# The SwiGLU product's blocks stored as high and low parts

## The chip, the cores and the metric

The kernel runs on one core of a Trainium2 chip. The metric is the device time of one execution in microseconds (us). Before the change three runs took 2479.89 to 2483.35 us, median 2483.05 us.

## The reference, cut to what matters

Two decoder layers act on x of shape 1024 x 1024 in float32. Each has a mixer, a cross attention into 256 memory tokens and a SwiGLU feed-forward stage, each followed by a layer norm of `ALPHA * x + f(x)`. The feed-forward stage is the one that the change touches:

```python
def swiglu_ffn(x, w_gate, w_up, w_down):      # w_gate, w_up: 1024 x 2816; w_down: 2816 x 1024
    return (jax.nn.silu(x @ w_gate) * (x @ w_up)) @ w_down
```

## The kernel before, in words

**Three matmuls for one.** Every float32 operand of a large product is split into a high part (a cast on ScalarE, ACT, to the rounded type float32r) and a low part (operand minus high part, on VectorE, DVE, or GpSimd, POOL). TensorE (PE) then does low*high, high*low and high*high into the same bank (`mm3`, L209 to L212). `split` (L214 to L216) makes the two parts.

**Seven products for eight.** Both matmul stages of the feed-forward use a two-by-two block scheme with seven block products; the operands of some of the seven are sums and differences of blocks.

**Gate and up stage** (`ffn`). The 22 feature chunks of 128 are worked through in 11 pairs c, one row chunk from each half. For one c, seven block products give the gate and seven give the up values, each of 12 matmuls (128x128 by 128x512). `operands` and `operand` make the weight operand of a product up to four products ahead (`while len(made) < min(4, left)`): DVE sums and differences (L1130 to L1139), an ACT cast (L1112), a DVE subtraction (L1113). `finish` empties the bank: ACT copies and silu, DVE additions and the product `hf`. Once all four blocks of `hf` exist, `store` (L1153) lets POOL make four sums and differences of 128x512 (L1159 to L1162); the seven resulting blocks go to DRAM, tile `hD`, in four transfers issued on ACT. These are deferred by `later` and `emit_later`, which runs once per block product here and once per group in the down stage.

**Down stage** (`ffn_down`, `seven`). The seven block products are taken in the order 1, 5, 6, 3, 7, 4, 2. Each is a block of six groups g (two feature chunks each, the last has one), and a group is 24 matmuls: 4 output tiles x 2 chunks x 3. A block product has 132 matmuls, the stage 924. For each group `operands7` takes the `hD` block by a load on SyncE's queue (SP; tile `raw`, in a pool of four buffers), has ACT cast it (`dh<-raw`, L215) and POOL subtract (`dl<-raw`, L216). It takes the weight block (`down_B`, tile `wp`): for products 1, 5, 6 and 4 a load of `in_wd`; for 5, 6, 7 and 4 a DVE difference of 128x1024 (L777, L783, L780, L786); then an ACT cast (`dh<-wp`) and a DVE subtraction (`dl<-wp`). The lookahead `look(j)` is 4 groups, 6 in products 4 and 2. During product 1 and 5 a `hook` also scales and shifts the eight residual tiles x (L1337, L1338), five on DVE and three on POOL.

**Order.** The order on each engine is that of the code, each engine works its queue in order, and semaphores join them. Everything but the residual pools lives in 44 pages of 4 KB per partition, and an instruction that writes a page waits for the last use of it.

Of the kernel before, what the change touches and what calls it, by code (L numbers as in the profile page):

```python
# [7 lines left out]
F32 = mybir.dt.float32  # L8
F32R = mybir.dt.float32r
# [6 lines left out]
P = 128  # L16
# [58 lines left out]
class Weights:  # L75
# [7 lines left out]
        self.split_ahead = 1  # L83
        self.lo_engine = ("vector",)

    def add(self, src, shape, scale=None, raw=False, page=False):
        self.items.append(dict(src=src, shape=shape, scale=scale, keep=raw or page, page=page))

    def load(self, parts=None):
        k, it = self.k, self.items[self.loaded]  # L90
        if it["page"]:
            it["raw"] = k.page(f"wp{self.loaded}", it["shape"])
        else:
            it["raw"] = k.raw.tile([P] + it["shape"], F32, tag="raw", name=f"raw{self.loaded}")
        if parts is None:
            k.nc.sync.dma_start(it["raw"], it["src"])
        else:
            for c in parts:
                k.nc.sync.dma_start(it["raw"][:, c, :], it["src"][:, c, :])
        self.loaded += 1  # L100
        return it["raw"]
# [43 lines left out]
class Kern:  # L145
    def __init__(self, ctx, tc, a):
        self.tc, self.nc, self.a = tc, tc.nc, a
        nc = self.nc
        self.pool = ctx.enter_context(tc.tile_pool(name="pages", bufs=a["n_pages"]))
        self.raw = ctx.enter_context(tc.tile_pool(name="rawp", bufs=4))  # L150
        dram = ctx.enter_context(tc.tile_pool(name="dram", bufs=1, space=bass.MemoryType.DRAM))
        self.xD = [dram.tile([P, D], F32, name=f"xD{t}") for t in range(NT)]
        self.hD = [dram.tile([7, P, min(2, HF - c), 512], F32, name=f"hD{c}") for c in range(0, HF, 2)]
        self.memT = [dram.tile([P, 4, MEM], F32, name=f"memT{q}") for q in range(2)]
        self.tmp = ctx.enter_context(tc.tile_pool(name="tmp", bufs=4))
        self.small = ctx.enter_context(tc.tile_pool(name="small", bufs=16))
        self.cst = ctx.enter_context(tc.tile_pool(name="cst", bufs=1))
        self.psum = ctx.enter_context(tc.tile_pool(name="psum", bufs=8, space=bass.MemoryType.PSUM))
        self.n = 0
        self.w = Weights(self)  # L160
        self.bg = []
        self.bg2 = []
        self.bg3 = []
        self.credit = [0.0, 0.0]
        self.later = []
        self.AT = [None, None]
# [937 lines left out]
    def ffn(self, layer):  # L1104
# [47 lines left out]

        def store(c, h):  # L1153

            a11, a21, a12, a22 = h[0][:, 0, :], h[0][:, 1, :], h[1][:, 0, :], h[1][:, 1, :]
            s12, s34 = self.page("s12", [2, 512]), self.page("s34", [2, 512])
            s1, s2, s3, s4 = s12[:, 0, :], s12[:, 1, :], s34[:, 0, :], s34[:, 1, :]
            gp = nc.gpsimd.tensor_tensor
            gp(s1, a21, a22, op=ALU.add)  # L1159
            gp(s3, a11, a21, op=ALU.subtract)  # L1160
            gp(s2, s1, a11, op=ALU.subtract)
            gp(s4, a12, s2, op=ALU.subtract)  # L1162
            dst = self.hD[c // 2][:, :, c % 2, :]

            def put(lo, src):
                return lambda: nc.scalar.dma_start(dst[lo:lo + src.shape[1]].rearrange("s p n -> p s n"), src)

            later.extend([(0, put(0, h[0][:, 0:1, :])), (0, put(1, h[1])), (3, put(3, s12)), (4, put(5, s34))])

        def finish(m, st, i, j, add, bank):  # L1170

# [126 lines left out]


    def down_operands(self):  # L1300
        return self.operands7(ORDER_D, lambda j, g: self.w.take(), self.down_B(self.nc.vector), len(self.hD))

    def ffn_down(self, layer):
        nc = self.nc
        self.w.split_ahead = 0
        self.w.lo_engine = ("gpsimd",)
        x = self.x = [None] * NT
        sts = [self.sm("lst", 5) for _ in range(NT)]
        gb, gx = [], []

        def norm_b(t):
            self.ln_b(x[t], sts[t], gb)
            if layer == DEPTH - 1:
                nc.sync.dma_start(self.a["out"][t * P:(t + 1) * P, :], x[t])

        def add(j, p, b):
            if j == 2 and p:
                norm_b(p - 1)
            self.add_block(j, b, x[p], x[p + 4], sts[p], sts[p + 4])
            if j == 4:  # L1320
                self.ln_a(x[p + 4], sts[p + 4])
            if j == 2:
                self.ln_a(x[p], sts[p])
                if layer < DEPTH - 1 and p < 2:
                    self.w.ahead(2 * p + 2, 2 * p + 4)

        def hook(j, g):
            self.emit_later()
            if j == 1 and g < 4:
                for t in (g, g + 4):  # L1330
                    x[t] = self.page("x", [D])
                    nc.sync.dma_start(x[t], self.xD[t])
            if j == 1 and g == 0:
                gx.extend(self.ln_params(self.a["ln_xa_g"][layer], self.a["ln_xa_b"][layer]))
            for t, eng in AFFINE.get((j, g), ()):
                eng = getattr(nc, eng)
                eng.tensor_tensor(x[t], x[t], gx[0], op=ALU.mult)  # L1337
                eng.tensor_tensor(x[t], x[t], gx[1], op=ALU.add)  # L1338
            if j == 4 and g == 0:
                gb.extend(self.ln_params(self.a["ln_ffn_g"][layer], self.a["ln_ffn_b"][layer]))  # L1340
            if j == 2 and 1 <= g < 5:
                norm_b(3 + g)

        self.seven(ORDER_D, self.down_made, self.down_ops, len(self.hD), HF, lambda j: 6 if j in (4, 2) else 4, add, hook, 1)
        self.down_ops = self.down_made = None
        self.last = (x[3], sts[3], gb)
        if layer == DEPTH - 1:
            x, st = x[3], sts[3]
            nc.vector.scalar_tensor_tensor(x, x, st[:, 2:3], gb[0], op0=ALU.add, op1=ALU.mult)
            for i, q in enumerate((nc.scalar, nc.sync)):  # L1350
                sl = slice(i * 512, i * 512 + 512)
                nc.vector.scalar_tensor_tensor(x[:, sl], x[:, sl], st[:, 4:5], gb[1][:, sl], op0=ALU.mult, op1=ALU.add)  # L1352
                q.dma_start(self.a["out"][3 * P:4 * P, sl], x[:, sl])
# [60 lines left out]
    def plan(self):  # L1414
        a, w = self.a, self.w

        def mem_k(l, extra=None, at=8):
            for q in range(2):
                w.add(self.memT[q], [4, MEM])
            for i in range(8):  # L1420
                if i == at:
                    extra()
                w.add(a["wk"][l, i], [8, P])

        def wout(eh):
            for kp in range(4):
                w.add(a["w_out"][eh, kp], [2, 512], page=True)

        def mem_v(l):
            for i in range(8):  # L1430
                w.add(a["wv"][l, i], [8, P])

        def attn(l):
            for i in range(8):
                w.add(a["wqT"][l, i], [8, P])
            for i in range(8):
                w.add(a["xa_wo"][l, i * P:(i + 1) * P, :], [D])

        def ffn(l):
            for c in range(2):  # L1440
                w.add(a["wg"][l, HF * c], [8, P])
                w.add(a["wu"][l, HF * c], [8, P])
            for m in range(2, NFF):
                for r in range(2):
                    w.add(a["wg" if m % 2 == 0 else "wu"][l, m // 2 + HF * r], [8, P], raw=True)
            for j in ORDER_D:
                for g, h in enumerate(self.hD):
                    w.add(h[DOWN_A[j]], [min(2, HF - 2 * g), 512], raw=True)
                    if j in DOWN_B:
                        r, c = DOWN_B[j]  # L1450
                        w.add(a["wd"][l, r, c, :, 2 * g:min(2 * g + 2, HF), :], [min(2, HF - 2 * g), 512], page=True)

        for i in range(24):
            w.add(a["w_in"][i], [8, P])
        mem_k(0, lambda: wout(0), 7)
        wout(1)
        for q in range(2):
            w.add(self.memT[q], [4, MEM])
        mem_v(0)
        attn(0)  # L1460
        ffn(0)
        mem_k(1)
        for i in range(2):
            w.add(a["pool_w"][i], [4, 256], (lambda i: lambda: self.pscale[:, i * 512:(i + 1) * 512].rearrange(
                "p (g c) -> p g c", c=256).unsqueeze(2).broadcast_to([P, 2, 2, 256]))(i))
        mem_v(1)
        attn(1)
        ffn(1)
# [120 lines left out]
```

## Time and profile before

| | |
|---|---|
| median of three runs | 2483.05 us |
| profiled execution | 2486.67 us, its span 2484.9 us |
| PE busy | 2325.7 us (94%) |
| DVE busy | 1842.3 us (74%) |
| ACT busy | 1050.7 us (42%) |
| POOL busy | 1044.8 us (42%) |
| DMA | 263.27 MB, mean 106 GB/s |

PE is the busiest engine, and its matmuls are pipelined: one is shown with 0.39 us but the next starts about 0.227 us later. So the time of a stage is read from the starts of its first and last matmul, not from busy time. An idle time is shown in brackets with the instruction that ended it. [...]

### The profile page before, as it was taken

Reading aid. Unit: us, or ns where it says so; the run is one execution under the profiler, and the core shown is the slowest. Engines: PE = TensorE matmul, PEld = TensorE weight load, DVE = VectorE, ACT = ScalarE, POOL = GpSimd, SP = SyncE. Lnnn points to the kernel's source line nnn. Section 1 sums busy time; section 2 is a strip of 40 time slices with the busy share of each in tenths; the row PEclk is TensorE's granted clock in tenths of the full one; section 3 lists DMA queues with packets and bytes.
Section 4 is the critical chain, followed back from the end, with each engine's and each line's share of the span. In section 5 each row is a group of like instructions: output and inputs, shape, how many; then the busy total and the mean of one; then the engine's idle time right before and its main releaser. Section 6 shows DMA issues by size and latency. Waiting matters only on the chain. (4 is left out here: it accounts for less than half of the span.)

```text
span 2484.9 us, 29326 instructions
## 1 busy us (share of the span) xinstructions
PE 2325.7 (94%) x11208; PEld 1920.4 (77%) x11208; DVE 1842.3 (74%) x1950; ACT 1050.7 (42%) x1723; POOL 1044.8 (42%) x573
## 2 busy tenths in 40 slices
PE   8999997798979999999989989798999999998997
PEld 6777776696868888888768789686788888886776
DVE  6986789877895766666788856979676666668877
ACT  3254564354736433333324443455454333332433
POOL 1332446666582112122556574666611211218654
PEclk9999999899989999999999999899999999999999
DMA  4211133150212133332734342302113323346342
GB/s 182 68 34 35 34 109 137 35 179 25 85 43 94 68 107 107 101 110 94 289 134 145 126 153 94 110 10 97 66 62 109 116 85 106 111 145 253 131 158 88
DMA packets 84476, 263.27 MB, mean 106 GB/s; under 512 B 8432, under 2 KB 8944, under 8 KB 84336
## 3 DMA queue, kind: packets, MB, share of 16 engines
q1 hardware_dynamic: 58464, 203.97, 24.2%
q10 hardware_dynamic: 25872, 57.42, 6.1%
q8 instruction: 89, 1.46, 0.3%
q14 instruction: 51, 0.42, 0.1%
HBM read 198.97 MB, written 62.39 MB: 105 GB/s over the span
## 5 line engine op out<-in xcount | busy, mean ns | idle before, releaser
L210 PE MATMUL D<-dh,dl 128*128 128x512 f32 x1176 | 471.4, 401 | 75.6 <-DVE x L247 39.1
L211 PE MATMUL D<-dl,dh 128*128 128x512 f32 x1176 | 471.4, 401 | 32.1 <-DVE dl L216 31.8
L212 PE MATMUL D<-dh,dh 128*128 128x512 f32 x1176 | 467.1, 397 | 0.0
L210 PE MATMUL P<-xh,op 128*128 128x512 f32 x1120 | 436.4, 390 | 2.3 <-ACT u L1274 1.4
L212 PE MATMUL P<-xh,op 128*128 128x512 f32 x1120 | 435.8, 389 | 0.0
L211 PE MATMUL P<-xl,op 128*128 128x512 f32 x1120 | 435.7, 389 | 0.0
L210 PEld LDWEIGHTS D<-dh,dl 128*128 128x128 f32 x1176 | 227.0, 193 | 132.6 <-issue 57.9
L216 POOL TENSOR_TENSOR dl<-raw,dh 128x1024 fp32r<-128x1024 f32 x84 | 233.5, 2796 | 184.8 <-ACT dh L215 177.8
L1159 POOL TENSOR_TENSOR s<-hf,hf 128x512 f32<-128x512 f32 x22 | 35.2, 1599 | 645.2 <-DVE hf L1185 371.3
L211 PEld LDWEIGHTS D<-dl,dh 128*128 128x128 f32 x1176 | 227.4, 193 | 87.3 <-DVE dl L216 40.5
L212 PEld LDWEIGHTS D<-dh,dh 128*128 128x128 f32 x1176 | 227.5, 193 | 47.9
L1113 DVE TENSOR_TENSOR op<-raw,op 128x512 fp32r<-128x512 f32 x200 | 139.5, 698 | 166.5 <-ACT op L1112 163.7
L216 DVE TENSOR_TENSOR dl<-wp,dh 128x1024 fp32r<-128x1024 f32 x96 | 189.3, 1988 | 81.6 <-ACT dh L215 65.2
L210 PEld LDWEIGHTS P<-xh,op 128*128 128x128 f32 x1120 | 210.3, 188 | 48.0 <-ACT u L1274 3.2
L211 PEld LDWEIGHTS P<-xl,op 128*128 128x128 f32 x1120 | 210.3, 188 | 43.8
L212 PEld LDWEIGHTS P<-xh,op 128*128 128x128 f32 x1120 | 210.3, 188 | 43.6
L125 POOL TENSOR_TENSOR wl<-raw,wh 128x1024 fp32r<-128x1024 f32 x64 | 172.4, 2706 | 166.7 <-ACT wh L123 166.4
L215 ACT CAST dh<-wp 128x1024 fp32r<-128x1024 f32 x96 | 94.8, 988 | 245.1 <-DVE wp L777 74.7
L365 DVE SCALAR_TENSOR_TENSOR cacc<-sig,par,cacc 128x1023 f32<-128x1023 f32 (+14 forms) x120 | 175.7, 1464 | 2.5
L1112 ACT CAST op<-raw 128x512 fp32r<-128x512 f32 x200 | 122.0, 620 | 110.9 <-DVE raw L1139 75.5
L216 POOL TENSOR_TENSOR dl<-xf,dh 128x1024 fp32r<-128x1024 f32 x48 | 141.5, 2964 | 39.7 <-ACT dh L215 29.2
L216 DVE TENSOR_TENSOR dl<-B,dh 128x1024 fp32r<-128x1024 f32 x48 | 117.9, 2489 | 40.9 <-ACT dh L215 40.9
(262 smaller groups left out, 4686.2 us busy)
## 6 DMA issues: line engine op xcount, KB each, us to landing
raw<-hD SPq DMA_DIRECT2D x70, 512.0 KB, 3.3
raw<-in_wg SPq DMA_DIRECT2D x44, 512.0 KB, 5.1
raw<-in_wu SPq DMA_DIRECT2D x44, 512.0 KB, 4.2
hD<-s ACTq DMA_DIRECT2D x44, 512.0 KB, 4.8
wp<-in_wd SPq DMA_DIRECT2D x40, 512.0 KB, 5.2
xD<-x ACTq DMA_DIRECT2D x32, 512.0 KB, 3.7
x<-xD SPq DMA_DIRECT2D x32, 512.0 KB, 6.8
raw<-in_w_in SPq DMA_DIRECT2D x23, 512.0 KB, 3.3
```

The costliest lines, as they stand in the source:

```text
L125: eng.tensor_tensor(lo, raw, hi.bitcast(F32), op=ALU.subtract)
L210: mm(out, ll, rh, start=start, stop=False, skip_group_check=more)
L211: mm(out, lh, rl, start=False, stop=False, skip_group_check=more)
L212: mm(out, lh, rh, start=False, stop=stop, skip_group_check=more)
L215: self.nc.scalar.copy(hi, src)
L216: getattr(self.nc, lo_engine).tensor_tensor(lo, src, hi.bitcast(F32), op=ALU.subtract)
L365: nc.vector.scalar_tensor_tensor(acc[:, s:], u[:, :S - s], w[:, j:j + 1], acc[:, s:], op0=ALU.mult, op1=ALU.add)
L1112: nc.scalar.copy(pg[:, 0], src)
L1113: getattr(nc, lo_engine).tensor_tensor(pg[:, 1], src, pg[:, 0].bitcast(F32), op=ALU.subtract)
L1159: gp(s1, a21, a22, op=ALU.add)
```

## The change

`store` now splits the seven blocks itself. For each c, ACT casts `h[1]`, `s12` and `s34` (128x1024 each, into new pages `sh`) and POOL subtracts in place (L1167 of the new file); block `a11` is split with a 128x512 cast into the page half of `a21`, which is no longer needed there, and a subtraction in place (L1171). `hD` has a leading index of two (low, high), and seven transfers in place of four carry both parts. In the last c the order differs so that block 0 is ready first. In the down stage each group loads two pages per `hD` block that go to PE as they are; the cast and the POOL subtraction of that side are gone. The loads come from the 44 pages in place of the raw pool, and the lookahead is 3 groups in products 6, 3 and 7 and 4 in the others.

```diff
-        self.hD = [dram.tile([7, P, min(2, HF - c), 512], F32, name=f"hD{c}") for c in range(0, HF, 2)]
+        self.hD = [dram.tile([2, 7, P, min(2, HF - c), 512], F32, name=f"hD{c}") for c in range(0, HF, 2)]
...
+            def split(k, src):
+                part[k] = self.page("sh", [2, 512], F32R)
+                nc.scalar.copy(part[k], src)
+                gp(src.bitcast(F32R), src, part[k].bitcast(F32), op=ALU.subtract)
+
+            def split11():
+                nc.scalar.copy(a21.bitcast(F32R), a11)
+                gp(a11.bitcast(F32R), a11, a21, op=ALU.subtract)
+
+            def put(to, src):
+                nc.scalar.dma_start(to.rearrange("s p n -> p s n"), src.bitcast(F32))
+
+            def put2(k, lo, src):
+                put(dst[1, lo:lo + 2], part.pop(k))
+                later.append((2, lambda: put(dst[0, lo:lo + 2], src)))
+
             gp(s1, a21, a22, op=ALU.add)
             gp(s3, a11, a21, op=ALU.subtract)
             gp(s2, s1, a11, op=ALU.subtract)
+            if last:
+                split11()
             gp(s4, a12, s2, op=ALU.subtract)
...
-            later.extend([(0, put(0, h[0][:, 0:1, :])), (0, put(1, h[1])), (3, put(3, s12)), (4, put(5, s34))])
+            n = (0, 1, 0, 1, 1, 2, 2) if last else (0, 1, 1, 2, 3, 3, 4)
+            for at, f in zip(n, (lambda: split(1, h[1]), lambda: put2(1, 1, h[1]),
+                                 lambda: (last or split11(), later.append((0 if last else 3, lambda: put(dst[:, 0], h[0])))),
+                                 lambda: split(3, s12), lambda: split(5, s34), lambda: put2(3, 3, s12), lambda: put2(5, 5, s34))):
+                later.append((at, f))
...
     def down_operands(self):
-        return self.operands7(ORDER_D, lambda j, g: self.w.take(), self.down_B(self.nc.vector), len(self.hD))
+        fb = self.down_B(self.nc.vector)
+        for j in ORDER_D:
+            for g in range(len(self.hD)):
+                r = [self.w.take() for _ in range(2)]
+                src = fb(j, g)
+                r += [self.page("dh", list(src.shape[1:]), F32R), self.page("dl", list(src.shape[1:]), F32R)]
+                self.split(r[2], r[3], src)
+                yield r
...
-        self.seven(ORDER_D, self.down_made, self.down_ops, len(self.hD), HF, lambda j: 6 if j in (4, 2) else 4, add, hook, 1)
+        self.seven(ORDER_D, self.down_made, self.down_ops, len(self.hD), HF, lambda j: 3 if j in (6, 3, 7) else 4, add, hook, 1)
...
-                    w.add(h[DOWN_A[j]], [min(2, HF - 2 * g), 512], raw=True)
+                    for part in (1, 0):
+                        w.add(h[part, DOWN_A[j]], [min(2, HF - 2 * g), 512], page=True, dt=F32R)
```

POOL's queue for one c in the middle of the gate and up stage of layer 0, before (s is s12 or s34, hf the product's pages), up to the first row of the next c:

```order
L1159 TENSOR_TENSOR s_1225_8267<-hf_8138,hf_8139 128x512
L1160 TENSOR_TENSOR s_1226_8268<-hf_8138 128x512
L1161 TENSOR_TENSOR s_1225_8267<-s_1225_8267,hf_8138 128x512
L1162 TENSOR_TENSOR s_1226_8268<-hf_8139,s_1225_8267 128x512
L1159 TENSOR_TENSOR s_1259_8541<-hf_8412,hf_8413 128x512
```

The same c after:

```order
L1180 TENSOR_TENSOR s_1243_8351<-hf_8221,hf_8222 128x512
L1181 TENSOR_TENSOR s_1244_8352<-hf_8221 128x512
L1182 TENSOR_TENSOR s_1243_8351<-s_1243_8351,hf_8221 128x512
L1185 TENSOR_TENSOR s_1244_8352<-hf_8222,s_1243_8351 128x512
L1167 TENSOR_TENSOR hf_8222<-hf_8222,sh_8375 128x1024
L1171 TENSOR_TENSOR hf_8221<-hf_8221 128x512
L1167 TENSOR_TENSOR s_1243_8351<-s_1243_8351,sh_8418 128x1024
L1167 TENSOR_TENSOR s_1244_8352<-s_1244_8352,sh_8439 128x1024
```

Four subtractions, three of them twice as wide, follow the four that were there.

ACT's queue behind the same point, before (op is a weight operand of a block product, u and sg are what empties a bank):

```order
L1274 COPY u_8293<-P_1230_8278 128x512
L1112 CAST op_8296<-raw_8077 128x512
L1178 ACTIVATE sg_8276<-sg_8276 128x512
L1112 CAST op_8315<-raw_7938 128x512
L1274 COPY u_8330<-P_1230_8278 128x512
L1112 CAST op_8332<-raw_8077 128x512
L1166 DMA hD_76<-s_1225_8267 128x2x512
L1274 COPY u_8349<-P_1237_8335 128x512
L1112 CAST op_8356<-raw_8079 128x512
```

And after:

```order
L1166 CAST sh_8375<-hf_8222 128x1024
L1296 COPY u_8378<-P_1248_8362 128x512
L1112 CAST op_8381<-raw_8157 128x512
L1174 DMA hD_76<-sh_8375 128x2x512
L1170 CAST hf_8221<-hf_8221 128x512
L1200 ACTIVATE sg_8360<-sg_8360 128x512
L1112 CAST op_8403<-raw_8008 128x512
L1166 CAST sh_8418<-s_1243_8351 128x1024
L1296 COPY u_8421<-P_1248_8362 128x512
L1112 CAST op_8423<-raw_8157 128x512
L1166 CAST sh_8439<-s_1244_8352 128x1024
L1174 DMA hD_76<-sh_8418 128x2x512
```

The new casts stand between the operand casts and the bank copies that PE's next products need.

SP's queue in the down stage of layer 0, product 6, before (hD_73 to hD_78 are the six groups' tiles):

```order
L96 DMA raw_9697<-hD_73 128x1024
L96 DMA wp_1441_9728<-in_wd 128x1024
L96 DMA raw_9734<-hD_74 128x1024
L96 DMA wp_1446_9767<-in_wd 128x1024
L96 DMA raw_9773<-hD_75 128x1024
```

And after:

```order
L96 DMA wp_1476_9860<-hD_73 128x1024
L96 DMA wp_1477_9862<-hD_73 128x1024
L96 DMA wp_1478_9864<-in_wd 128x1024
L96 DMA wp_1481_9897<-hD_74 128x1024
L96 DMA wp_1482_9899<-hD_74 128x1024
L96 DMA wp_1483_9901<-in_wd 128x1024
```

A group has three loads in place of two, all into pages.

## Rows read from the trace of the kernel before

**Rows 1.** First line of the page, and its row of an ACT cast.
```profile
span 2484.9 us, 29326 instructions
...
L1112 ACT CAST op<-raw 128x512 fp32r<-128x512 f32 x200 | 122.0, 620 | 110.9 <-DVE raw L1139 75.5
```

**Rows 2.** Timeline of PE, down stages: start, duration, operation, idle before and releaser.
```profile
1210.38 0.39 PE L210 MATMUL D<-dh,dl 128*128 128x512 f32 x1
...
1242.14 0.47 PE L210 MATMUL D<-dh,dl 128*128 128x512 f32 x1 [1.38 <-ACT dh L215]
...
1253.24 0.76 PE L210 MATMUL D<-dh,dl 128*128 128x512 f32 x1 [3.53 <-ACT dh L215]
...
1287.43 0.47 PE L210 MATMUL D<-dh,dl 128*128 128x512 f32 x1 [1.80 <-ACT dh L215]
...
1322.86 0.39 PE L210 MATMUL D<-dh,dl 128*128 128x512 f32 x1
...
1350.06 0.39 PE L210 MATMUL D<-dh,dl 128*128 128x512 f32 x1
...
1382.03 0.47 PE L210 MATMUL D<-dh,dl 128*128 128x512 f32 x1 [1.90 <-DVE x L247]
...
1443.34 0.39 PE L212 MATMUL D<-dh,dh 128*128 128x512 f32 x1
...
2237.45 0.39 PE L210 MATMUL D<-dh,dl 128*128 128x512 f32 x1
...
2470.73 0.39 PE L212 MATMUL D<-dh,dh 128*128 128x512 f32 x1
```

**Rows 3.** Stretches, layer 0: length, PE, PEld, DVE, ACT, POOL, PEclk, DMA share, GB/s.
```profile
1210.00:1240.00 30.00, 30.00 (x133) 24.52 (x132) 27.20 (x13) 7.99 (x9) 28.70 (x12) 1.00 0.92 351
1240.00:1287.00 47.00, 35.61 (x136) 26.70 (x134) 39.18 (x23) 11.88 (x13) 28.59 (x10) 0.93 0.45 162
...
1230.00:1235.00 5.00, 5.00 (x24) 4.14 (x23) 5.00 (x2) 0.00 (x0) 4.92 (x3) 1.00 1.04 419
...
1250.00:1255.00 5.00, 1.29 (x2) 0.79 (x3) 3.76 (x4) 1.99 (x2) 0.88 (x1) 0.82 0.33 107
1255.00:1260.00 5.00, 5.00 (x13) 3.92 (x12) 4.97 (x3) 0.00 (x0) 1.64 (x1) 0.50 0.46 165
```

**Rows 4.** Timeline of DVE, layer 0's down stage.
```profile
1229.05 2.88 DVE L216 TENSOR_TENSOR dl<-wp,dh 128x512 fp32r<-128x512 f32 x1
...
1288.53 3.42 DVE L783 TENSOR_TENSOR wp<-wp,wp 128x1024 f32<-128x1024 f32 x1
1293.20 1.23 DVE L216 TENSOR_TENSOR dl<-wp,dh 128x1024 fp32r<-128x1024 f32 x1 [1.25 <-issue]
...
1302.54 1.22 DVE L783 TENSOR_TENSOR wp<-wp,wp 128x1024 f32<-128x1024 f32 x1
...
1380.05 1.23 DVE L216 TENSOR_TENSOR dl<-wp,dh 128x1024 fp32r<-128x1024 f32 x1 [1.23 <-issue]
```

**Rows 5.** Timeline of POOL, the same stage.
```profile
1228.01 3.38 POOL L1337 TENSOR_TENSOR x<-x,lng 128x1024 f32<-128x1024 f32 x1
...
1288.31 2.56 POOL L216 TENSOR_TENSOR dl<-raw,dh 128x1024 fp32r<-128x1024 f32 x1 [4.40 <-ACT dh L215]
```

**Rows 6.** Waits of SP's queue, 1190 to 1230 us: in total, times, longest.
```profile
SPq L1332 <- DMA hD<-hf: 9.1, 1, 9.1
```

**Rows 7.** One stretch, the gate and up stage of layer 0.
```profile
833.00:1172.00 339.00, 338.24 (x1491) 279.77 (x1491) 215.16 (x286) 121.72 (x214) 60.32 (x37) 1.00 0.31 104
```

**Rows 8.** Timelines of POOL, DVE and PE behind one store in that stage.
```profile
1061.48 1.62 POOL L1162 TENSOR_TENSOR s<-hf,s 128x512 f32<-128x512 f32 x1
...
1061.87 1.77 DVE L1136 TENSOR_TENSOR raw<-raw,raw 128x512 f32<-128x512 f32 x1
...
1076.63 0.69 DVE L1113 TENSOR_TENSOR op<-s,op 128x512 fp32r<-128x512 f32 x1 [0.74 <-ACT op L1112]
...
1081.83 0.39 PE L210 MATMUL P<-xh,op 128*128 128x512 f32 x1
```

More of the change, by code (lines that the diff above doesn't have):

```diff
@@ L84, in __init__, with add @@
         self.lo_engine = ("vector",)
-    def add(self, src, shape, scale=None, raw=False, page=False):
-        self.items.append(dict(src=src, shape=shape, scale=scale, keep=raw or page, page=page))
+    def add(self, src, shape, scale=None, raw=False, page=False, dt=F32):
+        self.items.append(dict(src=src, shape=shape, scale=scale, keep=raw or page, page=page, dt=dt))
     def load(self, parts=None):
@@ L91, in load @@
         if it["page"]:
-            it["raw"] = k.page(f"wp{self.loaded}", it["shape"])
+            it["raw"] = k.page(f"wp{self.loaded}", it["shape"], it["dt"])
         else:
-            it["raw"] = k.raw.tile([P] + it["shape"], F32, tag="raw", name=f"raw{self.loaded}")
+            it["raw"] = k.raw.tile([P] + it["shape"], it["dt"], tag="raw", name=f"raw{self.loaded}")
         if parts is None:
-            k.nc.sync.dma_start(it["raw"], it["src"])
+            k.nc.sync.dma_start(it["raw"].bitcast(F32), it["src"])
         else:
@@ L1158, in store @@
             gp = nc.gpsimd.tensor_tensor
+            dst = self.hD[c // 2][:, :, :, c % 2, :]
+            last = c == HF - 1
+            part = {}
+            def split(k, src):
[10 more added lines that the diff above has]
+                later.append((2, lambda: put(dst[0, lo:lo + 2], src)))
             gp(s1, a21, a22, op=ALU.add)
@@ L1161, in store @@
             gp(s2, s1, a11, op=ALU.subtract)
+            if last:
+                split11()
             gp(s4, a12, s2, op=ALU.subtract)
-            dst = self.hD[c // 2][:, :, c % 2, :]
-            def put(lo, src):
-                return lambda: nc.scalar.dma_start(dst[lo:lo + src.shape[1]].rearrange("s p n -> p s n"), src)
-            later.extend([(0, put(0, h[0][:, 0:1, :])), (0, put(1, h[1])), (3, put(3, s12)), (4, put(5, s34))])
+            n = (0, 1, 0, 1, 1, 2, 2) if last else (0, 1, 1, 2, 3, 3, 4)
[3 more added lines that the diff above has]
+                later.append((at, f))
         def finish(m, st, i, j, add, bank):
```

## The prediction

> **What bounds the kernel now.** I read the page first, then the timeline of PE over the stages that the change touches, then the stretches around its gaps, and last the timelines of DVE and POOL beside them. The page's first line gives the span, 2484.9 us [rows 1]; the profiled execution took 2486.67 us, so 1.8 us lie around the span, and it is 3.6 us above the median of 2483.05. A difference under 0.2% (5 us) counts here as no change.
>
> PE bounds nearly everything, so I price a stage by what PE loses in it. Twelve matmuls into product 3 of the down stage the starts run from 1322.86 to 1350.06 us without a gap, 120 matmuls in 27.20 us, 0.2267 us each [rows 2]. A block product of 132 is then 29.92 us, and the 923 steps from a stage's first matmul to its last 209.2 us. Layer 0 takes 1210.38 to 1443.34, which is 232.96 us, and layer 1 2237.45 to 2470.73, 233.28 us [rows 2]. So the two down stages lose 23.7 and 24.0 us, 47.8 together: that is all the change can win there.
>
> Where layer 0 loses it follows from the same starts. Product 1: 1210.38 to 1242.14, 1.8 us over. Product 5: to 1287.43, 15.4 over. Product 6: product 3 begins 12 matmuls before 1322.86, at 1320.14, so 2.8 over. Product 3 none. Product 7: 1350.06 to 1382.03, 2.0 over, nearly all of it the one wait of 1.90 us for DVE. Products 4 and 2 together 1.7. In the stretch of product 5 PE is busy 35.61 of 47.00 us, 11.4 idle, of which 1.4 belong to the gap before the product; from there to 1260 the granted clock is 0.82 and then 0.50, the lower level, after the 3.53 us gap that ended at 1253.24 [rows 2, 3]. With the end of the gap at 1287.43, product 5's 15.4 us are 10.4 of waiting and 5.0 of lower clock.
>
> What ends the waits is the high part of a weight, cast by ACT, but behind it stands DVE. Its difference of 128x1024 takes 3.42 us at 1288.53 and 1.22 at 1302.54. The long one began beside a POOL subtraction that ran 1288.31 to 1290.87, and ended 1.1 us after it. The 128x512 subtraction at 1229.05 took 2.88 us beside POOL's operation of 1228.01 to 1231.39, and ended 0.5 us after it [rows 4, 5]. So such a DVE instruction stands still until POOL's is through. A group in product 5 or 6 needs the difference, 1.25 us in which DVE waits for the cast, and the subtraction of 1.23: 3.42 + 1.25 + 1.23 = 5.9 us beside POOL, and 3.7 us alone [rows 4]. PE wants a group each 24 x 0.2267 = 5.44 us. The chain is too slow by half a microsecond per group only because POOL makes the low part of the other operand.
>
> **The change, part by part: down stage.** The cast and the POOL subtraction of every hD group go, 42 of each per layer. After product 5 has begun, POOL then has nothing but the small statistics of the layer norm, and DVE's chain falls to 3.7 us, 1.7 below the need. Product 6's 2.8 us should go, and the 1.90 us before product 4 too: the subtraction that delayed DVE's residual addition there began at 1380.05 behind a chain of the long sort [rows 4]. What stays is the turn from product 1 to 5. POOL still has the last blocks' sums and subtractions and three residual tiles of two operations, 3.38 us each by the one row [rows 5], and these now end around 1245 rather than 1250. Replaying DVE by hand with these durations, PE still waits about 3.0 us for the first group of product 5, then 2.0 and 1.2, and a gap of that size gave the lower clock before, for which I leave 3.8 of the 5.0 us. Sum 10 per layer. Bounds: 4 us if DVE gets clear of POOL a group earlier (one wait and no lower clock), 16 if the turn stays as it is, which is product 5's 15.4 us. The gain is 47.8 - 20 = 27.8 us, between 16 and 40.
>
> SP's queue is the next thing to be late. Before, it waited 9.1 us for the last transfer into hD [rows 6]; now a cast and a subtraction come ahead of that transfer, so about 4 us later, and the weights of product 5 are queued behind it. The block itself is used by product 1's last group, 120 matmuls or 27 us into the stage, so it is early enough; the weights come around 1235, while DVE reaches them at 1237. I put it at nothing; cover gone, each microsecond of lateness is one of PE, within the 16 above.
>
> Loads: three of 0.52 MB per group in products 1, 5, 6 and 4, 1.57 MB in 5.44 us or 289 GB/s, and two in 3, 7 and 2. The queue has moved 351 GB/s over 30 us and 419 at a share of 1.04 [rows 3]. So they fit, with a margin of a fifth to a third. By the order of the instructions, and with before's PE times, each load is asked for 19 us or more ahead of its use. Nothing for it; the other end is a rival below.
>
> **Gate and up stage.** This is where the work goes. PE is busy 338.24 of 339.00 us there, DVE 215.16, ACT 121.72, POOL 60.32 [rows 7], so nothing is to be won and all can be lost. Per c (14 products of 12 x 0.2267 = 2.72 us, 38.1 us) ACT gets three casts of 128x1024 and one of 128x512. With 620 ns for 128x512 [rows 1], and at most double for twice the width, that is 4.3 us on an engine with 60% idle. POOL gets three subtractions of 2.56 us [rows 5] and one of about 1.3, 9.0 us, on an engine idle for most of the time. Their own time is hidden. Not hidden is what they do to DVE: its 1.77 us at 1061.87, beside POOL's sum that ended at 1061.48 + 1.62, again ended 0.5 us after POOL [rows 8]. DVE has 38.1 x (1 - 215.16/339.00) = 13.9 us idle per c. If each POOL subtraction stops it for all its length, 9.0 of these are used, within four or five products, whose own idle time is 4.5 x 1.0 us; the rest, 4.5 us, comes out of DVE's lead. That lead is 4.5 us behind a store: the operand's low part was ready at 1076.63 + 0.69, and PE took it at 1081.83 [rows 8]. So the margin is used up almost exactly. My replay of this one store leaves 0.3 us for that product and 0.7 to 1.3 for others. I take 0.2 us lost per c, 22 times over the two layers: 4 us. Bounds: nothing, and 3 us per c, 66 us, if each POOL subtraction takes the 3.38 us that a contended one takes [rows 5].
>
> [...]
>
> **Sum.** 2486.7 - 27.8 + 4 = 2462.9 us against the profiled execution, which is 3.6 above the median: 2459 us. The likeliest case's own range is 2446 to 2474, from 40 won and nothing lost to 16 won and 8 lost (2486.7 - 40 - 3.6 = 2443, and 2475; a little inside, since both ends at once are unlikely).
>
> **Rivals.**
> - *The down stages recover all.* DVE is clear of POOL in time for product 5: 2486.7 - 47.8 - 3.6 = 2435 us, or 2439 with the 4. For it speaks that DVE's chain alone is 3.7 us; against it, that POOL still has work in the first groups of the turn and that a single gap already lowered the clock.
> - *The loads become the bound.* hD is read twice as wide and 3 loads per group must come in time; the stretch from 1210 shows a share of 0.92 already [rows 3]. If each of the some 22 groups with three loads per layer waits 0.4 us, 18 us return: 2477, no more than a small gain. Against it: 289 of 351 GB/s.
> - *Gate and up stalls (slower).* POOL's subtractions stop DVE's operand sums, PE waits at each store. Beyond the 0.3 us that my replay leaves, each further microsecond is lost 22 times. With 2 us per c the stages lose 44: 2486.7 - 27.8 + 44 - 3.6 = 2499 us, and the lower clock would add to it. It cancels the gain from 1.3 us per c on. For it speak the rows of DVE ending behind POOL and the thin margin; against it, that POOL's four are spread over products, so DVE gets between them, and that part of DVE's work reads a bank and showed no such stop. With about 1.2 us per c it comes out at the time of before.
>
> **How the numbers follow.** Likeliest case 0.58; all recovered 0.12; loads the bound 0.08; gate and up stalling by over 1.4 us per c 0.15, by about 1.2 us 0.07. Faster takes the first two and three quarters of the third, 0.76; slower 0.15; the same 0.09. The range: 2438, since the first rival's lower half is left out, to 2487, which leaves out most of the slower one; some 0.18 outside.
>
> **What would show it.** Right: in the down stages no ACT or DVE wait of PE from product 6 on, DVE's difference at 1.22 us there, 132 matmuls in 29.9 us; product 5 still over by 5 to 12 us, with a wait at its first group; gate and up of one layer within 4 us of before. Wrong: waits of PE for ACT op casts behind each store in gate and up, with DVE rows of 2 to 4 us beside L1167; waits for a load in the down stage; a product 5 that is 15 us over still, or not over at all.

## The result, and the profile after

The changed kernel takes 2507.78 us (median of four runs, 2506.58 to 2508.28) against 2483.2 us of before on the same chip: a ratio of 1.0098, 95% interval 1.008 to 1.0115. It is slower by 24.6 us, and the forecast was 2459. The profiled execution's span is 2506.4 us, 21.5 longer than before [rows 1].

First the timeline of PE in the kernel after, at the ends of the stages (start, duration, operation, in brackets the idle time before and what ended it):

```profile
827.23 0.39 PE L210 MATMUL P<-xh,op 128*128 128x512 f32 x1
...
1236.75 0.39 PE L212 MATMUL P<-xh,op 128*128 128x512 f32 x1
1236.98 0.39 PE L210 MATMUL D<-dh,wp 128*128 128x512 f32 x1
...
1271.65 0.79 PE L210 MATMUL D<-dh,wp 128*128 128x512 f32 x1 [4.59 <-ACT dh L215]
1273.81 0.80 PE L211 MATMUL D<-dl,wp 128*128 128x512 f32 x1 [1.36 <-DVE dl L216]
...
1438.31 0.50 PE L211 MATMUL D<-dl,wp 128*128 128x512 f32 x1 [1.53 <-DVE dl L216]
...
1457.04 0.39 PE L212 MATMUL D<-dh,wp 128*128 128x512 f32 x1
...
2274.52 0.39 PE L210 MATMUL D<-dh,wp 128*128 128x512 f32 x1
...
2494.64 0.39 PE L212 MATMUL D<-dh,wp 128*128 128x512 f32 x1
```

The down stages take 1236.98 to 1457.04 and 2274.52 to 2494.64, 220.06 and 220.12 us, where they took 232.96 and 233.28 [rows 2]: 12.9 and 13.2 us won. The gate and up stage of layer 0 takes 409.52 us; before, its matmuls ran from 827.48 to 1210.15, 382.67 us. Layer 1 has 409.54 for 382.65. That is 26.9 us lost twice. Between and behind the stages another 6.2 us are won. The sum: 53.7 - 26.1 - 6.2 = 21.4 us, the difference of the spans but for rounding. The same two rows of the kernel before:

```profile
827.48 0.39 PE L210 MATMUL P<-xh,op 128*128 128x512 f32 x1
...
1210.15 0.39 PE L212 MATMUL P<-xh,op 128*128 128x512 f32 x1
```

The stage between them holds 1680 matmuls, which is ten c of 14 products. The first of the eleven c of a layer is made ahead of it by plain products (tile `pl`), so the two layers have 20 such c.

The loss comes with every c. The stretch of one c in the middle of the stage, before (us, then the busy time of PE, PE's loads, DVE, ACT and POOL, the granted clock PEclk, DMA share, GB/s):

```profile
1057.35:1095.43 38.08, 38.08 (x170) 31.54 (x168) 24.13 (x33) 13.68 (x24) 6.55 (x5) 1.00 0.31 104
```

And one c after:

```profile
909.50:950.28 40.78, 38.67 (x169) 31.38 (x168) 29.28 (x33) 16.94 (x28) 16.17 (x9) 1.00 0.41 142
```

DVE has the same 33 instructions and is busy 5.15 us longer: that is time in which it stood still. The granted clock is 1.00 in both, so the 2.7 us per c come from waits: PE is idle for 2.1 us, and by the starts of its matmuls each of its two waits costs some 0.3 us beyond the idle time shown, as the next two matmuls also start late. All waits of PE over eight c of the kernel after (in total, times, longest):

```profile
PE P L210 <- ACT u L1296: 15.2, 8, 1.9
PE P L210 <- DVE sg L1199: 1.1, 6, 0.2
```

Of before, the same question over its own eight c gives no wait at all. The one of 1.9 us is for `u`, the copy that ACT makes of a bank, not for an operand. How it comes about shows in the timeline of the kernel after behind one store, POOL first, then DVE, ACT and PE:

```profile
1037.70 2.73 POOL L1167 TENSOR_TENSOR hf<-hf,sh 128x1024 fp32r<-128x1024 f32 x1
1040.39 1.75 POOL L1171 TENSOR_TENSOR hf<-hf 128x512 fp32r<-128x512 f32 x1
...
1038.86 2.12 DVE L1113 TENSOR_TENSOR op<-raw,op 128x512 fp32r<-128x512 f32 x1 [0.69 <-ACT op L1112]
1040.90 0.68 DVE L1199 TENSOR_TENSOR sg<-P,u 128x512 f32<-128x512 f32 x1
1041.50 1.18 DVE L1139 TENSOR_TENSOR raw<-raw,s 128x512 f32<-128x512 f32 x1
...
1042.72 0.62 ACT L1112 CAST op<-raw 128x512 fp32r<-128x512 f32 x1 [0.47 <-DVE raw L1139]
1043.24 1.04 ACT L1166 CAST sh<-s 128x1024 fp32r<-128x1024 f32 x1
1044.19 0.58 ACT L1296 COPY u<-P 128x512 f32<-128x512 f32 x1
...
1044.82 0.50 PE L210 MATMUL P<-xh,op 128*128 128x512 f32 x1 [1.91 <-ACT u L1296]
```

DVE's subtraction of 0.69 us takes 2.12, until 0.55 us after POOL's L1167 is through (1040.43); its sum L1139 then takes 1.18 beside L1171. ACT's operand cast waits for that sum, the new cast of a block comes next in the queue, and the copy of the bank, whose product was done at 1040.0, stands behind both. PE adds its next product but one to that bank, so the copy has 2.72 us less its own 0.58, some 2.1 us, to spare; it starts 4.2 us after the bank was done.

### The profile page after: what moved, and what is told of

It reads as the page before. It is cut to its first block, busy times and chain, and to the rows that moved or that the text cites. A ratio compares the mean times of both kernels' runs of the same rounds, so it can differ in the third digit from the quotient of the medians.

```text
span 2506.4 us, 29564 instructions
## 1 busy us (share of the span) xinstructions
PE 2325.8 (93%) x11208; PEld 1916.3 (76%) x11208; DVE 1826.7 (73%) x1950; ACT 1049.4 (42%) x1727; POOL 1027.0 (41%) x577
## 5 line engine op out<-in xcount | busy, mean ns | idle before, releaser
L210 PE MATMUL P<-xh,op 128*128 128x512 f32 x1120 | 442.6, 395 | 40.4 <-ACT u L1296 37.7
L212 PE MATMUL P<-xh,op 128*128 128x512 f32 x1120 | 438.5, 392 | 0.0
L1113 DVE TENSOR_TENSOR op<-raw,op 128x512 fp32r<-128x512 f32 x200 | 231.0, 1158 | 154.6 <-ACT op L1112 103.3
L210 PE MATMUL D<-dh,dl 128*128 128x512 f32 x560 | 226.0, 404 | 58.3 <-DVE x L247 35.4
L210 PE MATMUL D<-dh,wp 128*128 128x512 f32 x616 | 241.6, 392 | 10.4 <-ACT dh L215 9.2
L211 PE MATMUL D<-dl,wp 128*128 128x512 f32 x616 | 241.8, 392 | 5.2 <-DVE dl L216 5.1
L211 PE MATMUL D<-dl,dh 128*128 128x512 f32 x560 | 224.5, 401 | 21.1 <-DVE dl L216 21.1
L212 PE MATMUL D<-dh,wp 128*128 128x512 f32 x616 | 240.7, 391 | 0.0
L216 DVE TENSOR_TENSOR dl<-wp,dh 128x1024 fp32r<-128x1024 f32 x96 | 142.5, 1493 | 117.8 <-ACT dh L215 75.6
L212 PE MATMUL D<-dh,dh 128*128 128x512 f32 x560 | 223.5, 399 | 0.0
L257 POOL TENSOR_SCALAR lst<-lst 128x1 f32<-128x1 f32 x48 | 27.3, 568 | 460.2 <-ACT sq L256 459.8
L210 PEld LDWEIGHTS D<-dh,dl 128*128 128x128 f32 x560 | 108.9, 195 | 85.4 <-issue 36.6
```

Source lines behind the costliest of these rows:

```text
L210: mm(out, ll, rh, start=start, stop=False, skip_group_check=more)
L211: mm(out, lh, rl, start=False, stop=False, skip_group_check=more)
L212: mm(out, lh, rh, start=False, stop=stop, skip_group_check=more)
L216: getattr(self.nc, lo_engine).tensor_tensor(lo, src, hi.bitcast(F32), op=ALU.subtract)
L257: nc.gpsimd.tensor_scalar(st[:, 3:4], st[:, 3:4], 1.0 / D, LN_EPS, op0=ALU.mult, op1=ALU.add)
L1113: getattr(nc, lo_engine).tensor_tensor(pg[:, 1], src, pg[:, 0].bitcast(F32), op=ALU.subtract)
```

## The experiments

The changed kernel and the twelve runs in one table; a c took 38.08 us before. Gate and up, and down, are of layer 0.

| kernel | median us | ratio to before, interval | gate and up | one c | down |
|---|---|---|---|---|---|
| after | 2507.78 | 1.0098 (1.008 to 1.0115) | 409.52 | 40.8 | 220.06 |
| e1_no_subs | 2445.82 | 0.9851 (0.9837 to 0.9866) | 385.53 | 38.4 | 213.78 |
| e2_copies_first | 2529.10 | 1.0187 (1.0169 to 1.0205) | 418.89 | 41.6 to 42.7 | 222.95 |
| e3_subs_dve | 2514.80 | 1.0129 (1.0113 to 1.0145) | 416.38 | 40.3, 41.8 | 217.70 |
| e4_dve_next | 2488.89 | 1.0027 (1.0016 to 1.0037) | 400.83 | 39.7 | 220.61 |
| f1_pool_late | 2464.85 | 0.9919 (0.9905 to 0.9934) | 381.94 | 38.08 | 225.89 |
| f2_dve_late | 2458.53 | 0.9894 (0.988 to 0.9909) | 381.95 | 38.08 | 223.41 |
| f3_pool_mid | 2501.37 | 1.0068 (1.0051 to 1.0084) | 401.41 | 39.9 | 224.18 |
| g1_refill_last | 2504.25 | 1.0089 (1.0074 to 1.0104) | 407.63 | 40.7 | 219.98 |
| g2_affine | 2499.75 | 1.0071 (1.0054 to 1.0088) | 407.60 | 40.7 | 218.30 |
| g3_look6 | 2493.73 | 1.0046 (1.0031 to 1.0061) | 407.64 | 40.7 | 216.68 |
| e5_two_subs | 2472.21 | 0.9953 (0.9938 to 0.9968) | 391.58 | 38.9 | 220.31 |
| h1_best | 2460.08 | 0.9903 (0.9887 to 0.992) | 381.94 | 38.08 | 224.72 |

**e1_no_subs.** POOL's subtractions taken out of the store:

```diff
-                gp(src.bitcast(F32R), src, part[k].bitcast(F32), op=ALU.subtract)
-                gp(a11.bitcast(F32R), a11, a21, op=ALU.subtract)
```

> The subtractions of the stored blocks' low parts are left out (the unsplit blocks are stored as the low parts); all casts, transfers and loads stay. The gate and up stages lost 53.7 us together against the kernel before, 2.72 us per c. Theory P, that POOL's subtractions stop DVE and so the operands and bank readings that PE waits for: the loss falls to under 0.3 us per c, 2507.8 - 47 = about 2460 us. Rival A, that ACT's new casts stand ahead of the bank copies in ACT's queue: little changes, 2495 to 2508 us. If both lie in one chain, with some 2 us of slack before PE feels it: also about 2460, since the casts alone (1.05 us each) stay within the slack.

The loss falls from 2.72 to 0.28 us per c, and the time is lower still than expected, since product 1 of the down stage loses nothing either (29.92 us, where after has 34.67). One c of this run:

```profile
1018.30:1056.66 38.36, 38.36 (x170) 31.47 (x169) 24.04 (x33) 16.90 (x28) 6.55 (x4) 1.00 0.44 151
```

ACT's time, with all the new casts, is that of after; DVE's is back at that of before. So the casts and transfers without the subtractions cost 0.3 us per c, and rival A is out as a sole cause.

**e2_copies_first.** The deferred work behind the emptying of the bank:

```diff
-            self.emit_later()
             if j in (1, 6, 5):
...
                 finish(m, st, 1, 0, None, b)
+            self.emit_later()
```

> The deferred work is put behind the emptying of the bank in each product's step, so that ACT copies a bank before it casts a block; POOL's subtractions stay. Theory P: 2500 to 2508 us, since DVE is stopped as before. Rival A: the 2.72 us per c go, 2450 to 2460 us. Both in one chain: the 1.05 us of one cast go from the wait of 1.91 us at the fourth product of each c, some 22 us in all, about 2485 us.

It is 21 us slower than after, which none of the three expected. The edit did another thing than I meant: `store` is called in `finish`, so a deferred step of distance 0 now comes in the same product's step, one product earlier. ACT's row in this kernel:

```profile
1035.22 0.62 ACT L1112 CAST op<-s 128x512 fp32r<-128x512 f32 x1 [7.51 <-DVE s L1133]
1037.58 1.05 ACT L1166 CAST sh<-hf 128x1024 fp32r<-128x1024 f32 x1 [1.74 <-DVE hf L1204]
1038.54 0.61 ACT L1112 CAST op<-s 128x512 fp32r<-128x512 f32 x1
```

The cast of the block waits 1.74 us for DVE's last product, with an operand cast queued behind it. So it tells nothing of the copies, but that earlier is worse.

**e3_subs_dve** (`gp` to `tt` in both subtractions) and **e4_dve_next** (the edit of e2, and each subtraction on DVE one product behind its cast; the diff shows this edit of e4 for one of the two lines):

```diff
-                gp(src.bitcast(F32R), src, part[k].bitcast(F32), op=ALU.subtract)
+                later.append((0, lambda: tt(src.bitcast(F32R), src, hi.bitcast(F32), op=ALU.subtract)))
```

> The same subtractions on DVE in place of POOL, at the same places. DVE gets 4.4 us more work per c (three of 1.23 and one of 0.69 us) and is no longer stopped for 9 us; but it waits in its queue for each cast, 1.25 us. Theory P: 2455 to 2470 us. Rival A: nothing gained, 2505 us or more, since the casts stay where they are and DVE now waits for them too. Both in one chain: 2465 to 2490.

> The two edits together (deferred work behind the bank's emptying, subtractions on DVE), and each subtraction one product later than its cast, so that DVE need not wait for it. Each theory expects the gate and up stages at the time of before or within 0.3 us per c: 2507.8 - 53.7 = 2454 to 2461 us, faster than both kernels. If it stays above 2480, the loss is neither ACT's order nor POOL's hold on DVE, but DVE's or the pages' load as such.

Neither does what theory P expected. With no hold by these subtractions at all, DVE's own 4.4 us at the same places still cost PE most of the loss: e3 loses 2.2 or 3.8 us per c, e4 1.6. The c of e3 from 1038.00 to 1078.30, which loses 2.2, has a granted clock of 1.00. That the others are 1.5 us longer by a lower clock is an estimate of mine, from the c of the kernel after with 0.96, which is 1.1 us longer than its neighbours (last section). The first c of e3 takes 47.65 us where before took 39.47, which no run explains. In e3 the first subtraction of a c also waits in DVE's queue for POOL's sums:

```profile
1045.52 1.23 DVE L1167 TENSOR_TENSOR hf<-hf,sh 128x1024 fp32r<-128x1024 f32 x1 [1.18 <-POOL s L1185]
1046.67 0.68 DVE L1136 TENSOR_TENSOR raw<-raw,raw 128x512 f32<-128x512 f32 x1
```

So it looks as if time taken from DVE at that place counts, be it a hold or work; the next three runs test that.

**f1_pool_late, f2_dve_late, f3_pool_mid.** Only the distances of the deferred steps change (f1 and f2; f3 has 3, 4, 5, 6, 8, 7, 9); f2 has DVE's subtractions as e4:

```diff
-            n = ... else (0, 1, 1, 2, 3, 3, 4)
+            n = ... else (4, 5, 6, 8, 11, 9, 12)
```

> The whole change with POOL's subtractions, but the four split steps of a c are put off to the 5th, 7th, 9th and 12th product behind the store, in place of the 1st, 2nd, 3rd and 4th (the last c as it was). Theory 'place': what counts is that DVE loses time right behind the store, where its sums of the next gate operands, POOL's four sums and the emptying of banks already meet, and where ACT's casts stand ahead of bank copies; elsewhere DVE has idle time between, and gate and up come back to 38.1 to 38.6 us per c: 2507.8 - 48 = about 2455 to 2462 us. Rival 'hold': each POOL subtraction holds DVE for its whole length and DVE's slack of about 2 us is overrun wherever it stands: 2490 us or more.

> The same late places, with the subtractions on DVE, each one product behind its cast. Theory 'place': 2452 to 2462 us, like the late POOL version or a little better, since nothing holds DVE and it only gains 4.4 us of work in 13.9 idle ones. Theory 'load' (DVE's added time as such is too much for its chain with ACT, wherever): 2480 us or more, as the early DVE version had 2488.9.

> POOL's subtractions at the 4th, 6th, 7th and 9th product behind the store, in between the early and the late places. Theory 'place': most of the loss is gone, 2455 to 2475 us, with a wait left where two subtractions follow closely. Rival 'hold': 2490 us or more. If the late version is slow and this one is fast, it is the pages held longer that cost, not the subtractions.

Late, both engines are free of loss: the first c takes 39.45 us (39.47 before) and each one behind it 38.08, with all the work of the change in it. One c of f1, f2 and f3, in this order:

```profile
1017.65:1055.73 38.08, 38.08 (x170) 31.54 (x169) 26.02 (x33) 16.80 (x28) 15.06 (x9) 1.00 0.43 152
1017.10:1055.18 38.08, 38.08 (x170) 31.53 (x169) 27.77 (x37) 16.90 (x28) 6.55 (x5) 1.00 0.43 152
1029.20:1069.20 40.00, 38.44 (x170) 31.45 (x168) 28.97 (x33) 16.80 (x28) 15.17 (x9) 1.00 0.42 145
```

'Place' holds for f1 and f2, and DVE's load as such is out, since f2's DVE is busy 27.77 us per c and PE waits for nothing. In f1 DVE is also held less, by 1.9 us per c (26.02 against 24.13) in place of 5.15, as 3.7 of the 8.5 us of POOL's late subtractions fall beside DVE's idle time and 2.1 beside its reads of a bank; so f1 alone does not part the place from the length of the hold. f3 does: its DVE is held nearly as long as that of after, 4.8 us, and only one of its holds costs PE anything. f3 fell short of what 'place' expected: 1.9 us per c are lost, all at one spot, the eleventh product. POOL, DVE, ACT and PE of f3 there:

```profile
1055.71 2.40 POOL L1167 TENSOR_TENSOR s<-s,sh 128x1024 fp32r<-128x1024 f32 x1 [2.83 <-ACT sh L1166]
...
1056.04 2.62 DVE L1207 TENSOR_TENSOR hf<-hf,sg 128x512 f32<-128x512 f32 x1
1058.58 0.68 DVE L1139 TENSOR_TENSOR raw<-raw,s 128x512 f32<-128x512 f32 x1
...
1059.29 0.62 ACT L1112 CAST op<-raw 128x512 fp32r<-128x512 f32 x1 [3.66 <-DVE raw L1139]
...
1060.22 0.59 ACT L1296 COPY u<-P 128x512 f32<-128x512 f32 x1 [0.32 <-ACT op L1112]
...
1060.86 0.50 PE L210 MATMUL P<-xh,op 128*128 128x512 f32 x1 [1.56 <-ACT u L1296]
```

It is the chain of after once more: one hold of DVE ahead of L1139, then the operand cast, then the copy. The three subtractions ahead of it, at 1040.90, 1046.22 and 1050.47, cost PE nothing. So 'place' is finer than "behind the store": it is the twice-a-c spot where L1139 feeds a cast that stands ahead of a bank's copy, and a hold of 1.9 us right before it (2.62 us in place of 0.69) was too long. In f1 the subtraction that falls there holds L1207 for 0.9 us only (1.63 us in place of 0.69, below), and PE waits for nothing.

**g1_refill_last.** The next operand is made behind the emptying of the bank:

```diff
-            while len(made) < min(4, left):
-                made.append(next(src))
...
+            while len(made) < min(3, left - 1):
+                made.append(next(src))
```

> The whole change as it is (POOL's subtractions, early places); alone the making of the next weight operand moves behind the emptying of the bank in each product's step, so that on ACT's queue the copy of a bank stands ahead of the operand cast that waits for DVE. Theory 'queue head': POOL's hold on DVE delays an operand cast that is not needed for three more products, and PE waits only because the bank copy stands behind that cast; with the copy ahead the loss of 2.72 us per c falls to under 0.5: 2507.8 - 43 or more, about 2455 to 2465 us. Rival 'late operands': PE would wait for the operands themselves, which now are asked for later: 2495 us or more.

My theory fell: 40.67 us per c, hardly less than 40.8. PE's waits over one c of g1:

```profile
PE P L210 <- ACT u L1294: 1.3, 2, 0.7
PE P L210 <- DVE sg L1199: 0.3, 1, 0.3
```

The wait of 1.9 us has become two of 0.7 and one of 0.3, and each of the three again costs some 0.3 us beyond its idle time. The copy of a bank still stands behind the operand cast of the step before. The order on ACT decides where the lateness shows; that DVE is late there decides that it shows.

**g2_affine** (in AFFINE, x4 to x7 on DVE at groups 1 to 4 of product 5) and **g3_look6** (`6 if j in (4, 2)`); g2 is on top of g1, and g3 on top of g2:

> The kernel with the operand made last, and in the down stage the scaling of the residual tiles x4 to x7 on DVE in groups 2 to 5 of product 5, instead of three of them on POOL in and after product 1. If the 4.7 us lost before product 5 and the 3.5 in it come from POOL's hold on DVE at that turn: 3 to 5 us gained per layer, 2446 to 2456 us. If they come from the loads behind the last transfer into hD: no gain, as the run beside it.

> The same, with the lookahead of before, six groups, in products 4 and 2. PE's 2.0 us of waits for DVE in product 2 go; the end of the layer norm behind the stage is paced by DVE, so between nothing and 4 us are gained against the run beside it, 1 by estimate; if the pages run short, it is slower.

g2 against g1 is 4.5 us faster in all, 1.7 and 1.9 us of it in the down stages. Product 1 falls to its 29.92, but product 6 now loses 2.8, which I put down to the added DVE work ending later. So POOL's work on the residual tiles was the cause of the wait before product 5, and of the 4.4 us gained there (the mean of the two layers) 2.8 are given back. g3 is 6 us faster than g2: product 2 takes, from its first start to its last, 29.69 instead of 32.08 us, so the 2.0 us of waits in it did count.

**e5_two_subs.** The two subtractions right behind POOL's sums left out (the one of `a11` likewise, by `if last`):

```diff
+                if k > 1 or last:
                     gp(src.bitcast(F32R), src, part[k].bitcast(F32), op=ALU.subtract)
```

> The changed kernel, early places, with two of its four POOL subtractions per c left out (those of block 1 and 2, 128x1024, and of block 0, 128x512; the unsplit blocks are stored as their low parts), in all c but the last. They stand right behind POOL's four sums; the two of s12 and s34 stay, two to four products later. Theory 'place': DVE is late because these two follow the sums without a pause, so most of the loss goes with them, 38.1 to 39 us per c, 2455 to 2470 us. Rival 'length': the loss goes by the length of POOL's holds, 3.8 of some 9 us, so about 1.5 us per c stay, 2475 to 2485 us.

0.86 us per c stay of 2.72, so two thirds of the loss come from these two, which have 4.48 of the 9.71 us that the four subtractions of a c take in the kernel after, or 46%. By the c that is what 'place' expected, by the time (2472) it lies between the two, since the down stage keeps its 220 us. PE's longest wait in two c is now 0.3 us.

**h1_best.**

> What the runs so far point to: the subtractions of all c but the last on DVE at the late places (the last as in the changed kernel), the residual tiles x4 to x7 scaled on DVE in product 5, six groups of lookahead in products 4 and 2. Gate and up at 381.9 us per layer as in the late DVE run, and the down stages at 216 to 220 us as in the run with six groups: 2458.5 less about 6 us per layer, 2443 to 2452 us, faster than both kernels. If the late places rather than the residual tiles delay product 5, its first wait stays near 9 us and the time near 2458.

It is no better than f2, and its 2460 us are near the second of the two outcomes that were expected. Gate and up are clean, but product 1 takes 37.49 us. SP's queue around the start of the down stage in h1 (who it waited for: in total, times, longest):

```profile
SPq L96 <- PE P L212: 20.2, 2, 17.7
SPq L96 <- DMA hD<-hf: 9.8, 1, 9.8
SPq L96 <- DMA hD<-sh: 7.2, 1, 7.2
```

And ACT there:

```profile
1238.32 0.62 ACT L215 CAST dh<-wp 128x512 fp32r<-128x512 f32 x1 [11.69 <-DMA wp<-in_wd]
```

The late steps of the last c but one store their blocks late: a load of product 1's third group waits 7.2 us for such a transfer (`hD<-sh`), and the loads behind it on SP come later too. ACT waits for a weight among these, so it issues a transfer of the last c (`hD<-hf`) 13.0 us into the down stage, where the kernel after does so 6.3 us into it. SP waits 9.8 us for that transfer, and the weight of product 1's last group is loaded behind it: that is ACT's 11.69 us. SP's longest wait, 17.7 us for PE to free a page, was over 16 us ahead of the stage. The chain is read from the trace of h1; no run tests it. The next step would be late places with the early ones in the last two c; that was not run. Of the kernels that do all the work f2 and h1 are the fastest, 1.1% and 1.0% faster than before, and their intervals overlap.

## Why the prediction was wrong

*The step that failed* is in the part on gate and up: "I take 0.2 us lost per c, 22 times over the two layers: 4 us". It measured 2.72 us in most c and 53.7 in all, over the 20 c that the two stages hold. The replay followed one thing, the lead of an operand's low part, and left it 0.3 us. PE does not wait for operands: it waits for the copy of a bank (L1296), which on ACT's queue stands behind an operand cast that waits for DVE. That path has some 2.1 us to spare, not the operand's 4.5 [rows 8]. The order of that queue is not the cause by itself: g1 changed it and still lost 2.6 us per c, with DVE held there too. The holds themselves were not over-large: DVE stood still 5.15 us per c, of the 9.0 that the bound had, and the 13.9 idle us would have covered them on average; e1, f1 and f2 show that no other part of the change costs gate and up more than 0.3 us per c.

*The rival that came true* is the slower one, 2499 us at 2 us per c, to which I gave 0.15. Its mechanism held (POOL's subtractions stop DVE, PE waits behind each store), with 2.7 us for the price and a copy in place of an operand sum. That DVE "gets between them" was the argument against it; e3 shows that even without a hold the place has no room.

*Which DVE instructions are held* shows in f1. Two rows of POOL there, and DVE's beside them:

```profile
1030.88 2.40 POOL L1167 TENSOR_TENSOR hf<-hf,sh 128x1024 fp32r<-128x1024 f32 x1 [7.38 <-ACT sh L1166]
...
1041.70 2.40 POOL L1167 TENSOR_TENSOR s<-s,sh 128x1024 fp32r<-128x1024 f32 x1 [3.00 <-ACT sh L1166]
...
1031.41 0.69 DVE L1199 TENSOR_TENSOR sg<-P,u 128x512 f32<-128x512 f32 x1 [0.89 <-PE P L212]
...
1043.01 1.63 DVE L1207 TENSOR_TENSOR hf<-hf,sg 128x512 f32<-128x512 f32 x1
```

L1199 reads a bank and took its usual 0.69 us inside the first. L1207, with both inputs in SBUF, lasted until 0.5 us after the end of the second at 1044.10. The gate and up stage of layer 0 in the kernel after shows the same: of DVE's single rows of 128x512 that began beside a POOL operation, the 21 that read a bank took 0.68 us each, and the 60 that read none 0.96 to 2.28. Alone, either kind took 0.68 to 0.70. The 60 ended 0.54 to 0.56 us after the POOL operation beside them, but for one beside a POOL row of two operations.

*The down stage* came out close to the forecast. It was to win 27.8 us and won 26.1. Products 6, 3, 7 and 4 take 29.92 us each; the difference L777 is long the last time beside POOL (L1366 from 1266.06 to 1269.38, L1367 from 1269.46 to 1272.67), and 1.22 us at this width from then on. Two rows of DVE in the kernel after:

```profile
1267.11 3.36 DVE L777 TENSOR_TENSOR wp<-wp,wp 128x1024 f32<-128x1024 f32 x1
...
1276.07 1.22 DVE L777 TENSOR_TENSOR wp<-wp,wp 128x1024 f32<-128x1024 f32 x1
```

The turn from product 1 to 5 has its wait, 4.59 and 1.36 us for the forecast 3.0, 2.0 and 1.2, and by its matmuls' starts product 5 loses another 2.2 us, at a lower clock, for the forecast 3.8. The stretch behind the long wait in the kernel after has a granted clock of 0.50, the prediction's lower level, as in [rows 3] from 1255 on:

```profile
1271.65:1276.65 5.00, 3.63 (x8) 2.55 (x9) 4.97 (x4) 0.00 (x0) 1.02 (x1) 0.50 0.63 247
```

Not forecast was that product 2 loses 2.5 us with the lookahead cut from six to four, as g3 shows; with it the stage stays 10.8 us over, where I had 10.

*The loads* were hidden, as taken: in layer 0's down stage of the kernel after neither PE nor DVE waits for a load, and ACT's one long wait, 9.4 us for the weight of product 1's last group, ended while DVE was still busy with other work. SP's wait for the last transfer was 8.9 us, where I had expected some 4 more than the 9.1 of [rows 6].

*Open.* How much of the 6.2 us won outside of the stages is the earlier end of DVE's work I did not test. Nor is it settled why the granted clock fell in some c and not in others with the same wait, or what delays the first c of e3.

## What to carry to other kernels

When work is added to an engine that has idle time on average, look for the path with the least to spare at the place where it is put, through every queue it goes, and not only for the data that the added work is near. Here the same instructions cost 53.7 us at one place and nothing a few products later. Deferring has its own price (in h1 product 1 of the down stage takes 37.49 us, where after has 34.67): the last of the deferred work must be back early where the next stage waits for it.

## What the runs showed of the hardware

Each c of the kernel after behind the first of its layer has a wait of 1.9 us. The granted clock is 1.00 in most of them (that of 40.78 us among these), but 0.96 in two of each layer, those from 867.63, 1072.67, 1905.15 and 2110.20 us. The first of them:

```profile
867.63:909.50 41.87, 39.96 (x170) 32.58 (x168) 29.19 (x33) 16.82 (x28) 16.20 (x9) 0.96 0.41 139
```

It takes 1.1 us longer than the next (41.87 for 40.78), though its one marked wait is the same 1.9 us. The down stage's wait of 4.59 us was followed by 0.50 from 1271.65 to 1276.65.

I had expected a hold of 9.0 us per c if every POOL subtraction stopped DVE fully. DVE gained 5.15 us of busy time. Some of its instructions there read a bank, and those took no longer beside POOL: in the kernel after L1199 took its 0.68 us at 1040.90 beside L1171, and in the kernel before the eight L1182 that read a bank between 833 and 1172 us took 0.68 us each beside POOL's sums. Part of POOL's time also falls where DVE is idle: 0.69 us of L1167 at 1037.70 and 0.96 us of the one at 1044.36.
